# Feed-forward products of a one-layer encoder step: the Strassen sums of the weight blocks move to VectorE, with one cast and one low part per k pair, and product banks in pairs

## The chip, the cores and the metric

The kernel runs on one core of one Trainium2 chip. The metric is the device time of one execution in microseconds (us). The kernel before took 3003.22 us, the median of three runs (3001.64 to 3003.44).

The core's engines run beside each other, each through its own list of instructions: PE (TensorE, matrix products), DVE (VectorE), ACT (ScalarE) and POOL (GpSimd) for elementwise work, and SP (SyncE), which issues most DMA transfers. Products are summed in PSUM, which here is used as eight banks of 512 float32 values in each of 128 partitions; the other tiles are in SBUF, and what doesn't fit goes to DRAM and back.

## The reference, cut to what matters

One layer of a streaming encoder, for 512 frames of a new stream and 16 frames of each of 8 running streams: 640 tokens in all, in float32. D_MODEL is 2048, D_FF is 5632, FFN_CONV is 3.

```python
def conv_ffn(h, conv_past, w_up, conv_w, w_down):
    gp, val = jnp.split(h @ w_up, 2, axis=-1)
    gc, conv_new = causal_conv(gp, conv_past, conv_w)
    return (jax.nn.silu(gc) * val) @ w_down, conv_new

def layer(x, ...):
    proj = rmsnorm(x, norm_mix_g) @ w_in
    ...
    x = x + concatenate([o_gdn, o_fox, o_lru]) @ w_out
    f_out, ffn_conv_new = conv_ffn(rmsnorm(x, norm_ffn_g), ...)
    return x + f_out, ...
```

A final RMSNorm follows. The mixers' caches and states and the last rows of `gp` are outputs too. The change touches only the two products of `conv_ffn` and what stands around them.

## The kernel before

**Tiling.** Features lie on the partitions: a feature tile is 128 features of all 640 tokens, kept as two halves of 320 tokens (HALF). A float32 matrix is split into a high part, rounded to float32r, and a low part, the rest; a product is three matmuls: high by high, high by low, low by high.

**Strassen's scheme in Winograd's form.** The two feed-forward products are cut into 2 x 2 blocks: the weights A by pair of output feature tiles and half of the inputs (K), the operand B by half of K and half of the tokens. Instead of eight block products there are seven, P1 to P7, each of a sum of weight blocks (S1 to S4 and some blocks as they are) by a sum of operand blocks (T1 to T4 and some blocks as they are); sums of the seven give the four output blocks. One step along K is a *k pair*: a tile of each half of K. It takes 7 x 3 = 21 matmuls of a 128 x 128 weight block by 128 x 320 operand (L1077). `SEQP` gives their order as (product, weight block, operand block).

**A k pair's weights** (`wino_w`, L1034 to 1055). SP loads four blocks, 512 columns (`w`). Three sums of 128 columns are made on Pool (L1047, 1049, 1052) and one on DVE (L1048), in a tile `ws`; ACT casts the three blocks that are used as they are (384 columns, L1050) and the four sums (512 columns, L1053) to the high part `wh`; DVE makes the two low parts `wl` (L1051, L1054). `next_w` keeps three pairs prepared.

**An operand set** (`wino_x`, L1009 to 1032) is one k pair of the operand: four blocks of 320 columns in `f`, four sums on Pool (L1013 to 1016), then a cast on ACT and a low part on DVE in three steps, of 640, 960 and 640 columns. `yield` ends a step: the generators that make operand sets are worked off a step at a time between the k pairs of the products (`drive`).

**The up products** (`up`, 44 passes, here called *feature tiles* or *up tiles*: each makes a gate tile and a value tile, from 8 k pairs). The 8 operand sets are made once (`form0`). At a tile's end ACT copies P1 and DVE adds the other products to it (five adds of 320 columns, and for the gate, `gate`, two of 256 and two of 64, which put the tokens where the convolution wants them). Pool multiplies by `corr`, a correction to the norm's factor (128 x 656), the width-3 convolution runs on ACT (L253) and DVE (two operations, L257), silu on ACT (L1358), again `corr` on Pool (L1359), and four DVE products give the result, which Pool's queue stores to `hT` in DRAM.

**The down products** (`form`, `down`). `form` loads tiles of `hT` and makes operand sets, of which at most 8 are on the chip. So each pair of output feature tiles is visited several times: a *pass* takes the k pairs that have come since its last visit. There are 32 passes, four rounds over 8 output pairs; the first 8 passes have 2, 3, 3, 4, 5, 6, 7 and 8 k pairs, and the list `ends` sets the rest. A pass loads the two tiles of the running sum from `x2` (DRAM) on SP (L1402), accumulates its products in PSUM, and adds them: ACT copies P1 (L1416), DVE makes eight adds of 320 columns (L1412 six times, L1418, L1419), Pool three (the helper at L1415), and SP stores the two tiles back to `x2` (L1430). The last eight passes keep their results on the chip. The tiles of `x` in a pass come from a pool of four buffers.

**The tail.** `plain` takes the last of the k pairs without Strassen's scheme, 12 matmuls for a half of the tokens, adds them (L1459), and collects the sums of squares; `finish` makes the final norm.

**PSUM.** From the up products on, all eight banks are one pool of single banks (`pf`, L1304); a tile or a pass takes seven.

**What sets the order.** The program is written in a tile framework: a pool gives a tile a buffer, and the framework makes a writer wait until the last reader of that buffer is done. The framework's scheduler sets the order of each engine's instructions ahead of the run: by and large the order of the code, but an operation whose data come later can be put behind a few that the code issues after it (DVE, for example, makes one pair's sum ahead of the low parts of the pair before). On the chip each engine keeps to its order. SP issues loads and stores in order as well, so a load that waits for a buffer holds those behind it. What the code issues between what is set by `next_w` inside `wino`, by the steps of `form0` or `form` between the k pairs (three steps in the up products, one in the down passes), and by the adds of a pass, which come after its products.

Of the kernel before, what the change touches and what calls it, by code (L numbers as in the profile page):

```python
# [50 lines left out]
class K:  # L51
    def __init__(self, ctx, tc, a, cfg):
# [208 lines left out]
    def load_x(self):  # L261
        """x * g in two parts; and the sums of x squared; yields k tile by k tile"""
# [7 lines left out]
        # the first two feature tiles' weights between the tiles of x: the second one's at half the pace  # L270
# [11 lines left out]
        # the sums of squares run behind: the odd tiles' on Pool, the even ones' on ACT and DVE  # L282
# [26 lines left out]
    def gates(self, ps):  # L309
        """softplus-based gates of GDN and FoX, their running sums, in the forms that the mixers use"""  # L310
# [16 lines left out]
        # softplus(z), token-major: z (16 columns per token block), -lambda of the LRU (4 columns)  # L327
# [44 lines left out]
        # the caches' log forget values: their sums  # L372
# [15 lines left out]
        # chunk sums of the GDN gates, running sums of the FoX ones  # L388
# [7 lines left out]
        # token-major: beta and G of the heads  # L396
# [8 lines left out]
        # exp(G), -beta exp(G), beta / 2  # L405
# [6 lines left out]
        # G of the last token of its chunk, for each token  # L412
# [11 lines left out]
        # the FoX sums as three bfloat16 parts  # L424
# [17 lines left out]
    def parts3(self, outs, x, tmp):  # L442
        """outs: three bfloat16 parts whose sum is -x"""
# [8 lines left out]
    def gdn_in(self, h, f0):  # L452
        """projections and convolutions of head h: 2 silu(.) of q, k, v, and of z"""
# [31 lines left out]
    def gdn(self, h, y, zs):  # L485
# [6 lines left out]
        # token-major, normalised, and back  # L492
# [22 lines left out]
        # decays  # L515
# [33 lines left out]
        # M, then A^T  # L549
# [19 lines left out]
        # (I + M)^-1 by doubling blocks: X the inverse, Z its transpose  # L569
# [428 lines left out]
    def fb(self):  # L998
        return self.ffn.tile([P, 4, HALF], F32, tag="f", bufs=3, name=self.name("f"))
# [741 lines left out]
```

## Time and profile before

| | before |
|---|---|
| median of three runs | 3003.22 us (3001.64 to 3003.44) |
| the profiled execution: its span, first to last instruction | 3000.6 us, the one time of it that is on record |
| mean granted TensorE clock | 0.983 of full speed |
| high by high and high by low of the feed-forward products (L1077, `wh`) | 7280 matmuls |
| low by high (L1077, `wl`) | 3640 matmuls |
| HBM traffic over the span | 122 GB/s |

The profile is of one execution. Its page gives the busy time of each engine, then the span in 40 equal slices of 75 us, with the busy share of each in tenths; "PEclk" is the clock that TensorE was granted. PEld is TensorE's weight load, which runs beside its matmuls. A row of the trace names the line of the kernel, the engine, the operation, and the tiles that it writes and reads ("wl<-ws,wh"), with partitions x columns and the type. A row of waits has the time an engine waited ahead of a line, the line that it waited for, the total, the count and the longest wait, in us. Windows are stretches of the span, with the busy time and the count of instructions of each engine.

By time the kernel has these stages: the input projection, the mixers and the output projection to 1232 us; the start of the up products to 1300; the up products to 2320; the first down passes to 2460; the middle ones to 2800; the last ones to 2936; the tail to the end.

### The profile page before, as it was taken

How to read it: one execution, taken by the hardware profiler on the slowest of the kernel's cores; microseconds unless marked ns; L12 is line 12 of the kernel's file. 1: busy time of each engine (PE TensorE's matmuls, PEld its weight loads, DVE VectorE, ACT ScalarE, POOL GpSimd, SP SyncE). 2: the span in 40 equal slices, each digit the busy share in tenths (PEclk: the TensorE clock that was granted, in tenths of full speed). 3: DMA queues.
4: the chain of work that ended last, by engine and by line, in shares of the span. 5: the costliest groups of instructions: out<-in, count | busy, mean ns of one | idle time of the engine just before them, and what ended most of it. 6: DMA issues, size and time to landing. Idle time of an engine off the chain costs nothing. (4 is left out here: it accounts for less than half of the span.)

```text
span 3000.6 us, 54322 instructions
## 1 busy us (share of the span) xinstructions
PE 2888.2 (96%) x19927; PEld 2804.4 (93%) x19927; DVE 2315.5 (77%) x3976; ACT 1109.7 (37%) x2023; POOL 1631.7 (54%) x2367
## 2 busy tenths in 40 slices
PE   8999999999999999999999999999999789999997
PEld 7999999999999999999999999999999789999996
DVE  8746545645634537899999999999999988999888
ACT  4333323323322313444444443444444334434433
POOL 3312200310300014677777777777777988888775
PEclk9999999999999999999999999999999899999998
DMA  5123143134134745433333333333333555555443
GB/s 207 56 93 109 59 143 121 59 123 143 58 109 150 264 130 179 130 105 98 98 99 101 98 98 103 99 101 98 98 98 98 171 160 156 164 163 173 155 138 119
DMA packets 175772, 369.68 MB, mean 123 GB/s; under 512 B 20137, under 2 KB 25145, under 8 KB 175505
## 3 DMA queue, kind: packets, MB, share of 16 engines
q1 hardware_dynamic: 169088, 340.28, 36.4%
q0 software_dynamic: 6416, 25.94, 2.4%
q8 instruction: 156, 2.56, 0.4%
q14 instruction: 112, 0.91, 0.1%
HBM read 306.75 MB, written 59.39 MB: 122 GB/s over the span
## 5 line engine op out<-in xcount | busy, mean ns | idle before, releaser
L1077 PE MATMUL p<-x,wh 128*128 128x320 f32 x7280 | 1625.0, 312 | 45.0 <-DVE t L1412 31.9
L1077 PEld LDWEIGHTS p<-x,wh 128*128 128x128 f32 x7280 | 1230.5, 190 | 56.4 <-DVE t L1412 36.2
L1077 PE MATMUL p<-x,wl 128*128 128x320 f32 x3640 | 1138.9, 313 | 8.9 <-DVE wl L1054 5.2
L1077 PEld LDWEIGHTS p<-x,wl 128*128 128x128 f32 x3640 | 691.5, 190 | 19.9 <-DVE wl L1054 15.1
L1054 DVE TENSOR_TENSOR wl<-ws,wh 128x512 fp32r<-128x512 f32 x520 | 527.4, 1014 | 25.3 <-ACT wh L1053 25.2
L1051 DVE TENSOR_TENSOR wl<-w,wh 128x384 fp32r<-128x384 f32 x520 | 449.6, 865 | 73.4 <-ACT wh L1050 67.7
L1053 ACT CAST wh<-ws 128x512 fp32r<-128x512 f32 x520 | 321.6, 619 | 389.4 <-POOL ws L1052 340.1
L146 PE MATMUL d<-xh,whi 128*128 128x320 f32 x1536 | 396.8, 327 | 0.0
L1050 ACT CAST wh<-w 128x384 fp32r<-128x384 f32 x520 | 264.8, 509 | 330.0 <-issue 169.8
L1052 POOL TENSOR_TENSOR ws<-w,ws 128x128 f32<-128x128 f32 x520 | 352.7, 678 | 40.4
L146 PE MATMUL d<-xl,whi 128*128 128x320 f32 x1536 | 370.8, 310 | 0.0
L146 PE MATMUL d<-xh,wlo 128*128 128x320 f32 x1536 | 370.5, 310 | 0.0
L1047 POOL TENSOR_TENSOR ws<-w 128x128 f32<-128x128 f32 x520 | 284.1, 546 | 150.3 <-DVE wl L1054 144.0
L1049 POOL TENSOR_TENSOR ws<-ws,w 128x128 f32<-128x128 f32 x520 | 344.0, 662 | 37.5
L135 DVE TENSOR_TENSOR wlo<-raw,whi 128x512 fp32r<-128x512 f32 x230 | 175.1, 761 | 212.5 <-ACT whi L134 204.8
L134 ACT CAST whi<-raw 128x512 fp32r<-128x512 f32 x230 | 142.4, 619 | 405.9 <-PE d L146 354.1
L146 PEld LDWEIGHTS d<-xh,whi 128*128 128x128 f32 x1536 | 256.9, 190 | 9.5 <-issue 5.5
L146 PEld LDWEIGHTS d<-xl,whi 128*128 128x128 f32 x1536 | 262.6, 189 | 0.2 <-issue 0.2
L146 PEld LDWEIGHTS d<-xh,wlo 128*128 128x128 f32 x1536 | 262.7, 189 | 0.0
L1048 DVE TENSOR_TENSOR ws<-w 128x128 f32<-128x128 f32 x520 | 218.3, 426 | 13.2 <-DMA w<-in_w_down 0.7
L868 POOL COPY q<-t 128x128 f32<-128x128 f32 x24 | 12.1, 523 | 261.2 <-DVE t L220 139.8
L257 DVE SCALAR_TENSOR_TENSOR t<-t,prm,t 128x656 f32<-128x656 f32 (+1 forms) x136 | 138.4, 1017 | 6.5 <-ACT t L253 3.5
(395 smaller groups left out, 3513.5 us busy)
## 6 DMA issues: line engine op xcount, KB each, us to landing
w<-in_w_up SPq DMA_DIRECT2D x352, 256.0 KB, 2.6
raw<-in_w_in SPq DMA_DIRECT2D x196, 256.0 KB, 2.8
w<-in_w_down SPq DMA_DIRECT2D x184, 256.0 KB, 2.7
t<-x SPq DMA_DIRECT2D x74, 320.0 KB, 3.6
kc<-in_ckT SPq DMA_DIRECT2D x32, 512.0 KB, 5.0
vc<-in_cv SPq DMA_DIRECT2D x32, 512.0 KB, 5.8
x<-t SPq DMA_DIRECT2D x48, 320.0 KB, 2.2
hT<-t POOLq DMA_DIRECT2D x44, 320.0 KB, 2.5
```

The lines of the kernel that those rows point to most:

```text
L134: nc.scalar.copy(hi[:, :n], raw[:, :n])
L135: nc.vector.tensor_sub(lo[:, :n], raw[:, :n], hi[:, :n].bitcast(F32))
L146: self.nc.tensor.matmul(ps[h][:, :HALF], wt[:, w], x[:, h * HALF:(h + 1) * HALF], start=start and i == 0, stop=stop and i == 2)
L1047: nc.gpsimd.tensor_add(s[:, 0], w[:, 0], w[:, 3])
L1048: nc.vector.tensor_sub(s[:, 2], w[:, 1], w[:, 0])
L1049: nc.gpsimd.tensor_sub(s[:, 1], s[:, 0], w[:, 1])
L1050: nc.scalar.copy(hi[:, 0:3], w[:, 1:4])
L1051: nc.vector.tensor_sub(lo[:, 0:3], w[:, 1:4], hi[:, 0:3].bitcast(F32))
L1052: nc.gpsimd.tensor_sub(s[:, 3], w[:, 2], s[:, 1])
L1053: nc.scalar.copy(hi[:, 3:7], s)
L1054: nc.vector.tensor_sub(lo[:, 3:7], s, hi[:, 3:7].bitcast(F32))
L1077: nc.tensor.matmul(ps[p], l[:, wi], r[:, xi], start=i == 0 and j == 0, stop=i == n - 1 and j == 2)
```

## The change

Seven products are still made for each k pair, of the same sizes and number of matmuls. What changes is who makes the sums, in how many operations, and in which PSUM banks the products lie.

- The scheme has other signs, so that two of the weight sums have a common minuend: one DVE operation of 256 columns makes both, and two DVE operations of 128 columns the other two. Pool makes none. The sums lie in the same tile as the loaded blocks (`w` now has 8 blocks, `ws` is gone), so that one ACT cast of 896 columns and one DVE low part of 896 columns serve all seven.
- `next_w` prepares sums and cast of a pair when it makes the low part of the pair before (`wn`).
- An operand set has its blocks and sums in one tile `f` of 7 blocks (two buffers, where there were three of 4 blocks and each set took two); cast and low part come in two steps, of 1280 and 960 columns, with a `yield` after each of the four operations.
- PSUM is split into four single banks (`pf1`: P1, P6, P7, the tail, and the other uses) and two tiles of two banks (`pf2`: P4 with P5, P2 with P3).
- In a down pass one tile with one buffer (`x2`, 128 x 1280) holds both tiles of the running sum, loaded by one DMA and stored by one. DVE's eight adds of 320 columns become four of 320 and two of 640; Pool's three become one of 640 and one of 320.
- The load of the convolution's past rows (`fc0`) is split into four; the host lays two weight blocks in another order; the number of bytes for DMA descriptors (`dynamic_dma_scratch_size`) is set to 4096. Comments and docstrings go, which shifts the line numbers.

```diff
-    SEQP = ((1, 0, 0), (6, 4, 5), (7, 5, 6), (5, 3, 4), (2, 1, 2), (4, 2, 1), (3, 6, 3))
+    SEQP = ((1, 0, 5), (6, 5, 1), (7, 3, 2), (5, 4, 0), (4, 1, 6), (2, 2, 3), (3, 6, 4))
     def fb(self):
-        return self.ffn.tile([P, 4, HALF], F32, tag="f", bufs=3, name=self.name("f"))
+        return self.ffn.tile([P, 7, HALF], F32, tag="f", bufs=2, name=self.name("f"))
...
     def pf1(self):
-        return self.pf.tile([P, 512], F32, tag="p", name=self.name("p"))
+        return self.pf.tile([P, 512], F32, tag="p", bufs=4, name=self.name("p"))
+    def pf2(self):
+        return self.pf.tile([P, 1024], F32, tag="pp", bufs=2, name=self.name("pp"))
     def wino_x(self, f, ready=lambda: True):
-        t = self.fb()
-        nc.gpsimd.tensor_sub(t[:, 0], f[:, 1], f[:, 0])
-        nc.gpsimd.tensor_sub(t[:, 1], f[:, 3], t[:, 0])
-        nc.gpsimd.tensor_sub(t[:, 2], f[:, 3], f[:, 1])
-        nc.gpsimd.tensor_sub(f[:, 1], f[:, 2], t[:, 1])
+        nc.gpsimd.tensor_sub(f[:, 0], f[:, 6], f[:, 5])
+        nc.gpsimd.tensor_add(f[:, 1], f[:, 4], f[:, 0])
+        nc.gpsimd.tensor_add(f[:, 2], f[:, 4], f[:, 6])
+        nc.gpsimd.tensor_sub(f[:, 6], f[:, 3], f[:, 1])
...
-        nc.scalar.copy(h3[:, 2:4], f[:, 2:4])
-        nc.vector.tensor_sub(l3[:, 2:4], f[:, 2:4], h3[:, 2:4].bitcast(F32))
-        yield
-        nc.scalar.copy(h3[:, 4:7], t[:, 0:3])
-        nc.vector.tensor_sub(l3[:, 4:7], t[:, 0:3], h3[:, 4:7].bitcast(F32))
-        yield
-        nc.scalar.copy(h3[:, 0:2], f[:, 0:2])
-        nc.vector.tensor_sub(l3[:, 0:2], f[:, 0:2], h3[:, 0:2].bitcast(F32))
+        for a, b in ((3, 7), (0, 3)):
+            nc.scalar.copy(h3[:, a:b], f[:, a:b])
+            yield
+            nc.vector.tensor_sub(l3[:, a:b], f[:, a:b], h3[:, a:b].bitcast(F32))
+            yield
     def wino_w(self, src, plain):
-        w = self.wf.tile([P, 4, P], F32, tag="w", bufs=4, name=self.name("w"))
-        s = None if plain else self.wf.tile([P, 4, P], F32, tag="ws", bufs=2, name=self.name("ws"))
+        w = self.wf.tile([P, 8, P], F32, tag="w", bufs=4, name=self.name("w"))
...
-        nc.gpsimd.tensor_add(s[:, 0], w[:, 0], w[:, 3])
-        nc.vector.tensor_sub(s[:, 2], w[:, 1], w[:, 0])
-        nc.gpsimd.tensor_sub(s[:, 1], s[:, 0], w[:, 1])
-        nc.scalar.copy(hi[:, 0:3], w[:, 1:4])
-        nc.vector.tensor_sub(lo[:, 0:3], w[:, 1:4], hi[:, 0:3].bitcast(F32))
-        nc.gpsimd.tensor_sub(s[:, 3], w[:, 2], s[:, 1])
-        nc.scalar.copy(hi[:, 3:7], s)
-        nc.vector.tensor_sub(lo[:, 3:7], s, hi[:, 3:7].bitcast(F32))
-        return hi, lo
+            nc.vector.tensor_tensor(w[:, 4:6], w[:, 0:1].to_broadcast([P, 2, P]), w[:, 1:3], op=OP.subtract)
+            nc.vector.tensor_sub(w[:, 6], w[:, 1], w[:, 5])
+            nc.vector.tensor_sub(w[:, 7], w[:, 3], w[:, 6])
+            part = w[:, 1:8]
+        n = part.shape[1]
+        nc.scalar.copy(hi[:, 0:n], part)
+        return part, hi, lo
+    def wino_lo(self, part, hi, lo):
+        n = part.shape[1]
+        self.nc.vector.tensor_sub(lo[:, 0:n], part, hi[:, 0:n].bitcast(F32))
+        return hi, lo
     def next_w(self):
         while len(self.wq) < 3:
-            src = next(self.wseq, None)
-            if src is None:
+            if self.wn is None:
+                src = next(self.wseq, None)
+                self.wn = src and self.wino_w(*src)
+            if self.wn is None:
                 break
-            self.wq.append(self.wino_w(*src))
+            now, src = self.wn, next(self.wseq, None)
+            self.wn = src and self.wino_w(*src)
+            self.wq.append(self.wino_lo(*now))
         return self.wq.pop(0)
     def wino(self, n, xops, make=None, base=0, done=None):
-        ps = {p: self.pf1()[:, :HALF] for p, _, _ in self.SEQP}
+        one = {p: self.pf1() for p in (1, 6, 7)}
+        two = [self.pf2().rearrange("p (a c) -> p a c", a=2) for _ in range(2)]
+        ps = {p: t[:, :HALF] for p, t in one.items()}
+        ps[45], ps[23] = [t[:, :, :HALF] for t in two]
+        for p, t in ((4, 45), (5, 45), (2, 23), (3, 23)):
+            ps[p] = ps[t][:, p % 2 if t == 23 else p - 4]
...
-        nc.gpsimd.dma_start(ns_fc[:, :, 1:, :], a["fc0"])
+        for f in range(0, NF, 11):
+            nc.gpsimd.dma_start(ns_fc[:, f:f + 11, 1:, :], a["fc0"][:, f:f + 11])
...
         def down(i, end, make):
             last = end == nw
+            xx = k.xt() if last else k.ffn.tile([P, 2 * NTOK], F32, tag="x2", bufs=1, name=k.name("x2"))
             if last:
-                fin[i] = k.xt()
-            xs = [fin[i][:, e * NTOK:(e + 1) * NTOK] if last else k.t() for e in range(2)]
-            for e in range(2):
-                nc.sync.dma_start(xs[e], x2[2 * i + e])
+                fin[i] = xx
+            x = xx[:, :2 * NTOK].rearrange("p (e h c) -> p e h c", e=2, h=2)
+            nc.sync.dma_start(x.rearrange("p e h c -> p e (h c)"), x2[2 * i:2 * i + 2].rearrange("e p t -> p e t"))
...
-            add(0, 0, ps[1])
+            nc.vector.tensor_add(x[:, 0, 0], x[:, 0, 0], ps[1])
             nc.vector.tensor_add(u2, u2, ps[6])
             nc.vector.tensor_add(u3, u2, ps[7])
-            add(0, 1, ps[5])
-            add(1, 1, ps[5])
-            add(0, 0, ps[2])
-            add(1, 0, ps[4])
-            add(0, 1, ps[3])
-            gadd(1, 1, u3)
-            gadd(1, 0, u3)
-            gadd(0, 1, u2)
+            nc.vector.tensor_add(x[:, 1], x[:, 1], ps[45])
+            nc.vector.tensor_add(x[:, 0, 1], x[:, 0, 1], ps[5])
+            nc.vector.tensor_add(x[:, 0], x[:, 0], ps[23])
+            nc.gpsimd.tensor_tensor(x[:, 1], x[:, 1], u3.unsqueeze(1).to_broadcast([P, 2, HALF]), op=OP.add)
+            nc.gpsimd.tensor_add(x[:, 0, 1], x[:, 0, 1], u2)
             if not last:
-                for e in range(2):
-                    nc.sync.dma_start(x2[2 * i + e], xs[e])
+                nc.sync.dma_start(x2[2 * i:2 * i + 2].rearrange("e p t -> p e t"), x.rearrange("p e h c -> p e (h c)"))
```

More of the change, by code (lines that the diff above doesn't have):

```diff
@@ L988, in load_o, with fpart @@
             yield
-    SEQP = ((1, 0, 0), (6, 4, 5), (7, 5, 6), (5, 3, 4), (2, 1, 2), (4, 2, 1), (3, 6, 3))
+    SEQP = ((1, 0, 5), (6, 5, 1), (7, 3, 2), (5, 4, 0), (4, 1, 6), (2, 2, 3), (3, 6, 4))
     def fb(self):
-        return self.ffn.tile([P, 4, HALF], F32, tag="f", bufs=3, name=self.name("f"))
+        return self.ffn.tile([P, 7, HALF], F32, tag="f", bufs=2, name=self.name("f"))
+    @staticmethod
+    def fpart(f, j):
+        return f[:, 5 - 2 * j:7 - 2 * j, :].rearrange("p a c -> p (a c)")
     def xt(self, dt=F32):
@@ L1037, in wino_w @@
         nc = self.nc
[L1038 to L1039 removed]
+        w = self.wf.tile([P, 8, P], F32, tag="w", bufs=4, name=self.name("w"))
         hi = self.wf.tile([P, 7, P], F32R, tag="wh", bufs=3, name=self.name("wh"))
         lo = self.wf.tile([P, 7, P], F32R, tag="wl", bufs=3, name=self.name("wl"))
[L1042 removed]
+        nc.sync.dma_start(w[:, 0:4].rearrange("p a c -> p (a c)"), src)
         if plain:
[L1044 to L1054 removed]
+            part = w[:, 0:4]
+        else:
+            nc.vector.tensor_tensor(w[:, 4:6], w[:, 0:1].to_broadcast([P, 2, P]), w[:, 1:3], op=OP.subtract)
[8 more added lines that the diff above has]
+        self.nc.vector.tensor_sub(lo[:, 0:n], part, hi[:, 0:n].bitcast(F32))
         return hi, lo
@@ L1303, in body @@
         k.mix = k.ffn
-        k.pf = ctx.enter_context(tc.tile_pool(name="pf", bufs=8, space=PSUM, reuse_waits="tile"))
+        k.pf = ctx.enter_context(tc.tile_pool(name="pf", bufs=4, space=PSUM, reuse_waits="tile"))
         def spread(r, out):
@@ L1389, in form @@
                 hi, lo = [x[:, :4 * HALF].rearrange("p (a c) -> p a c", c=HALF) for x in op]
-                nc.scalar.copy(hi, f)
+                nc.scalar.copy(hi, f[:, 3:7])
                 yield
-                nc.vector.tensor_sub(lo, f, hi.bitcast(F32))
+                nc.vector.tensor_sub(lo, f[:, 3:7], hi.bitcast(F32))
                 hops.append((hi, lo))
@@ L1408, in down @@
             u2, u3 = u[:, :HALF], u[:, HALF:NTOK]
-            x = {(e, h): xs[e][:, h * HALF:(h + 1) * HALF] for e in range(2) for h in range(2)}
-            def add(e, h, b):
-                nc.vector.tensor_add(x[e, h], x[e, h], b)
-            def gadd(e, h, b):
-                nc.gpsimd.tensor_add(x[e, h], x[e, h], b)
             nc.scalar.copy(u2, ps[1])
-            add(0, 0, ps[1])
+            nc.vector.tensor_add(x[:, 0, 0], x[:, 0, 0], ps[1])
             nc.vector.tensor_add(u2, u2, ps[6])
             nc.vector.tensor_add(u3, u2, ps[7])
-            add(0, 1, ps[5])
-            add(1, 1, ps[5])
-            add(0, 0, ps[2])
-            add(1, 0, ps[4])
-            add(0, 1, ps[3])
-            gadd(1, 1, u3)
-            gadd(1, 0, u3)
-            gadd(0, 1, u2)
+            nc.vector.tensor_add(x[:, 1], x[:, 1], ps[45])
[3 more added lines that the diff above has]
+            nc.gpsimd.tensor_add(x[:, 0, 1], x[:, 0, 1], u2)
             if not last:
-                for e in range(2):
-                    nc.sync.dma_start(x2[2 * i + e], xs[e])
+                nc.sync.dma_start(x2[2 * i:2 * i + 2].rearrange("e p t -> p e t"), x.rearrange("p e h c -> p e (h c)"))
         blocks = (0, 128, HALF - 128)
@@ L1451, in plain @@
                     n = 0
-                    for kh, wi in enumerate(((1, 2), (0, 3))[e]):
+                    for kh, wi in enumerate(((1, 3), (0, 2))[e]):
                         for l, r in ((hi, xh), (hi, xl), (lo, xh)):
-                            nc.tensor.matmul(ps[e], l[:, wi], r[:, 2 * kh + h], start=n == 0, stop=n == 5)
+                            nc.tensor.matmul(ps[e], l[:, wi], r[:, 2 - 2 * kh + h], start=n == 0, stop=n == 5)
                             n += 1
@@ L1511, in weights @@
                     yield a["w_down"][i, nw], True
-        k.wseq, k.wq = weights(), []
+        k.wseq, k.wq, k.wn = weights(), [], None
         for f in range(NF - 1):
```

14 lines of the change are left out of this document (5 added, 9 removed).

## The prediction

> **What bounds the kernel now.** I read the page first, for shares and slices.
>
> ```profile
> span 3000.6 us, 54322 instructions
> PE 2888.2 (96%) x19927; PEld 2804.4 (93%) x19927; DVE 2315.5 (77%) x3976; ACT 1109.7 (37%) x2023; POOL 1631.7 (54%) x2367
> PE   8999999999999999999999999999999789999997
> DVE  8746545645634537899999999999999988999888
> POOL 3312200310300014677777777777777988888775
> PEclk9999999999999999999999999999999899999998
> ```
>
> PE is full almost everywhere; the one dip (slices 32 and 33) has a lower granted clock and a Pool at nine and eight tenths. Next the windows by stage: start of the up products, up products, first down passes, middle ones, last ones, tail.
>
> ```profile
> 1232.00:1300.00 68.00, 62.30 (x409) 60.55 (x409) 60.73 (x104) 31.50 (x54) 54.25 (x81) 0.97 0.31 92
> 1300.00:2320.00 1020.00, 1017.64 (x6878) 1008.53 (x6878) 970.17 (x1598) 412.08 (x777) 785.99 (x1273) 1.00 0.34 100
> 2320.00:2460.00 140.00, 112.78 (x658) 107.06 (x657) 129.08 (x189) 56.08 (x99) 126.42 (x156) 0.89 0.51 165
> 2460.00:2800.00 340.00, 319.99 (x2081) 314.00 (x2080) 305.00 (x459) 137.48 (x253) 288.02 (x392) 0.97 0.52 161
> 2800.00:2936.00 136.00, 136.00 (x930) 136.00 (x929) 115.87 (x207) 49.98 (x96) 97.36 (x151) 1.00 0.45 144
> ```
>
> After the stretch and its length stand PE, weight loads, DVE, ACT and Pool with their counts, then the clock. The up products run 6878 matmuls in 1020 us, 6.74 a us. At that rate the first down passes would hold 944 and have 658: 42.4 us lost. The middle ones would hold 2293 and have 2081: 31.4 us lost. The start loses 7.3 us. So some 81 us can be won in these stages; up and last passes hold PE at its own pace. The waits of PE between 2320 and 2800 say what ends last:
>
> ```profile
> PE p L1077 <- DVE t L1412: 31.9, 16, 3.5
> PE p L1077 <- ACT wh L1050: 5.1, 3, 2.3
> ```
>
> At 16 pass ends PE waits 2.0 us for the adds that free the product banks, so DVE is behind. The loss has two parts: PE idle, 27.2 and 20.0 us by the windows, and the clock that drops after a stop, 0.11 x 140 = 15 and 0.03 x 340 = 10 us. So a stop that goes takes half its length again with it. DVE is behind because it shares its time with Pool:
>
> ```profile
> 1817.37 1.86 POOL L1354 TENSOR_TENSOR t<-t,corr 128x656 f32<-128x656 f32 x1 [1.55 <-DVE t L1344]
> 1817.67 2.10 DVE L1054 TENSOR_TENSOR wl<-ws,wh 128x512 fp32r<-128x512 f32 x1
> ```
>
> An operation that takes 0.68 at best (below) lasted until Pool's was done.
>
> **Costs of one operation.** Minimum, median, maximum by line:
>
> ```profile
> L1048 DVE TENSOR_TENSOR ws<-w x520: 276/433/970, 1216.4 to 2924.1; 128x128 f32<-128x128 f32 x174
> L1051 DVE TENSOR_TENSOR wl<-w,wh x520: 543/812/1760, 1226.5 to 2929.3; 128x384 fp32r<-128x384 f32 x174
> L1054 DVE TENSOR_TENSOR wl<-ws,wh x520: 676/946/2114, 1227.0 to 2930.3; 128x512 fp32r<-128x512 f32 x174
> L1412 DVE TENSOR_TENSOR t<-t,p x144: 472/475/482, 2363.6 to 2838.9; 128x320 f32<-128x320 f32 x144
> L1047 POOL TENSOR_TENSOR ws<-w x520: 446/506/1369, 1216.2 to 2924.4; 128x128 f32<-128x128 f32 x174
> L1014 POOL TENSOR_TENSOR f<-f,f x29: 857/1169/1460, 1152.5 to 2772.3; 128x320 f32<-128x320 f32 x29
> L1359 POOL TENSOR_TENSOR t<-t,corr x44: 1338/1344/1352, 1279.7 to 2366.1; 128x656 f32<-128x656 f32 x44
> L1463 POOL TENSOR_TENSOR x<-x,t x10: 1540/1606/2011, 2945.0 to 2972.5; 128x640 f32<-128x640 f32 x10
> ```
>
> DVE's minima lie on 143 ns + 1.042 ns a column. Four rows give the spacing (start, duration): independent neighbours start 0.39 apart at 0.48 long, so 0.09 overlaps; an operation that waits for the one before starts 0.04 after its end.
>
> ```profile
> 2938.70 0.48 DVE L1412 TENSOR_TENSOR x<-x,p 128x320 f32<-128x320 f32 x1
> 2939.09 0.48 DVE L1419 TENSOR_TENSOR u<-u,p 128x320 f32<-128x320 f32 x1
> 2984.68 0.16 DVE L114 TENSOR_TENSOR s<-s 128x3 f32<-128x3 f32 x1
> 2984.88 0.16 DVE L115 SCALAR_TENSOR_TENSOR s<-s,s 128x3 f32<-128x3 f32 x1
> 2934.96 0.31 PE L1077 MATMUL p<-x,wl 128*128 128x320 f32 x1
> 2935.40 0.31 PE L1077 MATMUL p<-x,wl 128*128 128x320 f32 x1
> ```
>
> The last two are three matmuls apart: 0.1467 each, 3.08 us for the 21 of a k pair, 24.64 for a feature tile of 8 pairs.
>
> **Weight blocks, per k pair.** Removed: three Pool sums (3 x 0.446 = 1.34 us undisturbed), one DVE sum and two low parts (0.276 + 0.543 + 0.676 - 3 x 0.09 = 1.225). Added on DVE: a sum of 256 columns (no such row; 0.41 by the line, between the 128 and 384 rows' 0.276 and 0.543), two of 128, one low part of 896 columns (1.08 by the line, beyond its longest row; the two removed ones together were 1.22). That is 2.04 us of durations. The second and third sum each wait for the one before. DVE in the steady part of an up tile, before:
>
> ```order
> L1048 TENSOR_TENSOR ws_18666<-w_18665 128x128
> L1051 TENSOR_TENSOR wl_18634<-w_18631,wh_18633 128x384
> L1054 TENSOR_TENSOR wl_18634<-ws_18632,wh_18633 128x512
> L1048 TENSOR_TENSOR ws_18700<-w_18699 128x128
> L1051 TENSOR_TENSOR wl_18668<-w_18665,wh_18667 128x384
> L1054 TENSOR_TENSOR wl_18668<-ws_18666,wh_18667 128x512
> ```
>
> and now (w holds the blocks and their sums, wl the low part):
>
> ```order
> L1051 TENSOR_TENSOR w_16918<-w_16918 128x256
> L1052 TENSOR_TENSOR w_16918<-w_16918 128x128
> L1053 TENSOR_TENSOR w_16918<-w_16918 128x128
> L1061 TENSOR_TENSOR wl_16860<-w_16858,wh_16859 128x896
> L1051 TENSOR_TENSOR w_16948<-w_16948 128x256
> L1052 TENSOR_TENSOR w_16948<-w_16948 128x128
> ```
>
> Here the waiting sums follow directly; elsewhere others stand between. Taken as half and half: 2.04 - 3 x 0.09 + 0.04 = 1.80 us, between 1.68 (none adjacent) and 1.94 (all). So DVE alone gets 0.58 us more per pair, Pool 1.34 less. What Pool costs DVE decides.
>
> **Up products.** The other DVE work of a tile is 15 operations (five adds of 320 columns, two each of 256 and 64, the conv's two of 656, four products of 256 and 64), by the line and the spacing 5.3 us. Before: 8 x 1.225 + 5.3 = 15.1 alone; Pool 8 x 1.34 + 3.6 (two of 656 columns at 1.34, and 0.9 put down for small copies) = 14.3; DVE was busy 970/1020 of 24.64 = 23.4. So a share (23.4 - 15.1)/14.3 = 0.58 of Pool's time lands on DVE. After: 8 x 1.80 + 5.3 + 0.58 x 3.6 = 21.8, with all of Pool's time 23.3: below 24.64 either way. PE stays the bound: -1 us (it idles 2.4 in the stage).
>
> At a tile's end the banks go in pairs: P4 and P5 come free together after five adds, P2 and P3 after the gate's. PE after three products of a new tile, before:
>
> ```order
> L1077 MATMUL p_19412<-x_11700,wh_19315 128x320
> L1077 MATMUL p_19412<-x_11701,wh_19315 128x320
> L1077 MATMUL p_19412<-x_11700,wl_19316 128x320
> L1077 MATMUL p_19413<-x_11700,wh_19315 128x320
> L1077 MATMUL p_19413<-x_11701,wh_19315 128x320
> ```
>
> and now:
>
> ```order
> L1094 MATMUL p_18644<-x_11859,wh_18557 128x320
> L1094 MATMUL p_18644<-x_11860,wh_18557 128x320
> L1094 MATMUL p_18644<-x_11859,wl_18558 128x320
> L1094 MATMUL p_18645<-x_11859,wh_18557 128x320
> L1094 MATMUL p_18645<-x_11860,wh_18557 128x320
> L1094 MATMUL p_18645<-x_11859,wl_18558 128x320
> L1094 MATMUL p_18646<-x_11859,wh_18557 128x320
> L1094 MATMUL p_18646<-x_11860,wh_18557 128x320
> L1094 MATMUL pp_18647<-x_11702,wh_18527 128x320
> ```
>
> Instead of the fourth product stand eight matmuls of the second pair's single products, so the paired bank (pp) is wanted 17 x 0.147 = 2.5 us into the tile. P1 ends 2.6 us before the old tile does, and seven adds and two sums of about 0.4 each run from then: done at about +1.2, or +2.2 with a low part in front. Covered; uncovered, each 0.5 us of lateness would cost 43 x 0.5 = 21 us.
>
> **Middle down passes.** Counts in a stage, by the windows of one line: low parts (pairs), the second u sum (passes) and the 960-column low part (operand sets), then the pairs of the first passes.
>
> ```profile
> 2460.00:2800.00 340.00, 82.03 (x99) 0.97 0.52 161
> 2460.00:2800.00 340.00, 7.14 (x15) 0.97 0.52 161
> 2460.00:2800.00 340.00, 15.08 (x13) 0.97 0.52 161
> 2320.00:2460.00 140.00, 26.17 (x32) 0.89 0.51 165
> ```
>
> Operands of a set: one cast less, low parts 1.48 + 1.14 - 0.18 = 2.44 on DVE for 2.49; two more turns between steps, hidden, since a set is used for the first time only every sixth pair or so. Adds of a pass: eight of 320 (3.1 us) become four and two of 640 (0.81 by the line): 3.0. Pool's three adds of 0.87 become 1.54 + 0.87. Before, as pairs + passes + sets: DVE alone 99 x 1.225 + 15 x 3.1 + 13 x 2.49 = 200, Pool alone 99 x 1.34 + 15 x 2.6 + 13 x 3.43 = 216 (four sums of 0.857 a set), busy 305: share (305 - 200)/216 = 0.49. After: DVE 99 x 1.80 + 15 x 3.0 + 13 x 2.44 = 255; Pool 15 x 2.4 + 45 = 81. DVE: 255 + 0.49 x 81 = 294, between 255 and 336. PE needs 305. DVE was filled to 0.90; without Pool's chain in front of the casts I take 0.95, 310 us, and leave 8 us for stops: 318, **-22 us**.
>
> **First down passes** (32 pairs, 6 passes, 8 sets and the last tile's 5.3 us). Before, casts stood behind Pool:
>
> ```profile
> 2335.09 0.99 ACT L1027 CAST x<-f 128x960 fp32r<-128x960 f32 x1 [7.04 <-POOL f L1014]
> ```
>
> That wait goes with the weight sums that stood ahead on Pool. By the same sum DVE alone was 83 and Pool 90, busy 129 (share 0.51). Now DVE alone is 32 x 1.71 (few sums adjacent here) + 18 + 19.5 + 5.3 = 97 and Pool 14.5 + 27.5 + 3.6 = 46: 97 + 0.5 x 46 = 120, between 97 and 143; filled to 0.95 that is 127 for 140. Against it: x2 has one buffer, so a pass's x is loaded only after the last one's is stored.
>
> ```profile
> x<-t SPq DMA_DIRECT2D x48, 320.0 KB, 2.2
> t<-x SPq DMA_DIRECT2D x74, 320.0 KB, 3.6
> vc<-in_cv SPq DMA_DIRECT2D x32, 512.0 KB, 5.8
> ```
>
> Adds 2.4, Pool 2, store 2.2 to 4, load 3.6 to 6: 10 to 14 us a round. Passes of 6 pairs (18.5 us) cover it, those of 3, 3 and 4 pairs (9.2, 9.2, 12.3) don't: 0 to 11 us, partly inside DVE's 127. Behind the waiting load SP holds the weight loads, but it runs some six pairs ahead, which covers 14 us; behind an add that waits for x DVE holds the next pairs' sums and low parts, and PE waits for those. I take 5 of the 13 back: **-8 us**.
>
> **The rest.** Start: Pool's chain gone, -2 (-7 to +5). Last passes: 45 pairs x 1.80 + 9 x 3.0 + 0.4 x 22 of Pool's adds = 117 us of DVE, for 116 now, in 136: 0. Tail: single banks fall from 8 to 4, so PE can be only one pair ahead.
>
> ```profile
> 2947.09 0.87 DVE L1459 TENSOR_TENSOR x<-x,p 128x320 f32<-128x320 f32 x2
> 2947.88 1.27 DVE L1045 TENSOR_TENSOR wl<-w,wh 128x512 fp32r<-128x512 f32 x1
> 2949.07 0.87 DVE L1459 TENSOR_TENSOR x<-x,p 128x320 f32<-128x320 f32 x2
> ```
>
> DVE takes 1.98 us a pair, PE 12 x 0.147 = 1.76; tied together for 16 pairs: +4 (0 to +8). ACT's casts shrink and wait less; ACT is never the bound. Splitting the fc0 load and the smaller descriptor ring touch nothing on the path: 0.
>
> Sum: -2 - 1 - 8 - 22 + 4 = -29; 3000.6 - 29 = 2971.6. The median lies 2.6 above the profiled span: **2974 us**.
>
> **Rivals.**
> A (0.60): the sum above; its own range 2955 to 2992.
> B (0.14): PE becomes the bound in the down passes too, as DVE's 294 for 305 allows: -42 - 31 - 5 - 1 + 2 = -77: 2926. Against it: DVE stays above 0.9.
> C (0.12): the pass ends are late as before, since their adds are no shorter and DVE is as full: 2997 to 3009.
> D (0.14), slower: all of Pool's time lands on DVE. Filled to 0.97, the middle takes 336/0.97 = 346 (+6), the first passes 143/0.97 + 8 = 155 (+15), tail +6: 3000.6 + 27 + 2.6 = 3030. Break-even over both stages, at a fill of 0.95 and with the +4 and -3 of the rest: (479 x 0.95 - 255 - 97)/(81 + 46) = a share of 0.81; the stages show 0.49 to 0.58, which is why D gets no more.
> The Trainium skill, SBUF — State Buffer, "Who interferes with whom", speaks for D: a DVE instruction with two SBUF inputs and a GpSimd instruction that reads SBUF exclude each other, and the second to issue is fully blocked. The rows of 1817 agree; the shares stay below 1 since Pool also runs beside adds that read PSUM.
>
> A change under 0.2% (6 us) can't be told from none. Faster A and B: 0.74; same C: 0.12; slower D: 0.14. The range reaches halfway from A into D and most of the way to B: 2935 to 3016.
>
> **What would show it.** Right: up stage at 6.7 matmuls a us with DVE near 0.9; low part near 1.08 us; middle near 318 us. Wrong: a DVE pair above 2.4 us, PE waits on paired banks in the up tiles, or PE waits after x loads.

## The result and the profile after

The changed kernel took 3034.47 us (median of four runs, 3032.94 to 3035.66) where the kernel before took 3003.33: a ratio of 1.0104, 95% interval 1.009 to 1.0118. It is 1% slower; 2974 had been forecast, with a range that ended at 3016.

First the page of the changed kernel: span, engines, and three rows of slices.

```profile
span 3033.9 us, 51647 instructions
PE 2888.9 (95%) x19927; PEld 2794.8 (92%) x19927; DVE 2281.2 (75%) x4403; ACT 1048.3 (35%) x1474; POOL 727.1 (24%) x778
PE   7999999999999998999999999999999789999996
DVE  8746545644643537898889888898898998999887
POOL 3312200300310013222222223222222433322114
```

Pool has lost 905 of its 1632 us. DVE, which took over its sums, is no busier than before (2281 for 2316). PE does the same matmuls in the same busy time, and the span is 33 us longer: PE waits more. Next the windows by stage, cut where PE starts the same matmul as at the cuts of before (there at 1232.1, 1300.1 and 2936.1 in place of the round times), so each holds the same products as the rows in the prediction. The columns are again length, PE, weight loads, DVE, ACT, Pool, clock.

```profile
1237.80:1302.80 65.00, 61.38 (x409) 60.47 (x408) 58.46 (x118) 28.36 (x33) 16.98 (x25) 0.97 0.33 95
1302.80:2338.80 1036.00, 1020.38 (x6878) 1008.39 (x6877) 923.02 (x1926) 378.45 (x450) 255.43 (x292) 1.00 0.34 98
2338.80:2473.20 134.40, 109.89 (x658) 104.55 (x657) 124.79 (x198) 50.65 (x59) 60.26 (x54) 0.91 0.47 159
2473.20:2818.00 344.80, 317.05 (x2082) 308.06 (x2081) 311.33 (x519) 124.77 (x142) 93.47 (x76) 0.99 0.49 160
2818.00:2967.30 149.30, 139.59 (x930) 136.15 (x930) 127.30 (x226) 44.83 (x54) 24.94 (x20) 1.00 0.43 136
```

Against before: +5.7 us ahead of the first cut, -3 in the start, **+16.1 in the up products**, -5.6 in the first down passes, +4.8 in the middle ones, **+13.2 in the last ones** (136.1 before, with no idle time of PE at all), +2.1 in the tail. In none of the three long stages is DVE full: 923 of 1036, 311 of 345, 127 of 149. The waits of PE in the changed kernel (total, times, longest) say what it lacks; line 1369 is an add at a tile's end in `up`, lines 1427 to 1432 are the adds of a down pass, "pp" is a pair of banks:

```profile
PE pp L1094 <- DVE x L1432: 21.4, 26, 1.0
PE p L1094 <- DVE x L1427: 16.6, 11, 4.4
PE pp L1094 <- DVE t L1369: 11.6, 20, 1.2
PE pp L1094 <- DVE x L1431: 7.9, 15, 0.6
```

All four are banks that come free late, three of them paired ones. One tile's end on DVE and PE (start, duration, line; DVE's sums of 128 columns are left out). Its last stop is one of the longer ones: PE waits for line 1369 at 20 tile ends, 0.6 us each on average.

```profile
1821.75 0.43 DVE L1051 TENSOR_TENSOR w<-w 128x256 f32<-128x256 f32 x1 [2.09 <-DMA w<-in_w_up]
1822.75 1.08 DVE L1061 TENSOR_TENSOR wl<-w,wh 128x896 fp32r<-128x896 f32 x1
1823.75 0.42 DVE L1051 TENSOR_TENSOR w<-w 128x256 f32<-128x256 f32 x1
1824.74 1.08 DVE L1061 TENSOR_TENSOR wl<-w,wh 128x896 fp32r<-128x896 f32 x1
1825.74 0.48 DVE L1364 TENSOR_TENSOR t<-t,p 128x320 f32<-128x320 f32 x1
...
1828.68 0.48 DVE L1369 TENSOR_TENSOR t<-t,pp 128x320 f32<-128x320 f32 x1
```

```profile
1824.76 0.45 PE L1094 MATMUL p<-x,wh 128*128 128x320 f32 x2
1826.28 0.55 PE L1094 MATMUL p<-x,wh 128*128 128x320 f32 x2 [0.47 <-DVE t L1364]
1829.21 0.56 PE L1094 MATMUL pp<-x,wh 128*128 128x320 f32 x2 [1.06 <-DVE t L1369]
```

PE begins the new tile at 1824.76. DVE, which stood idle for 2.09 us up to 1821.75 because the weights of a later pair had not landed, then makes sums and low part of two later pairs, and comes to the first add 1.0 us *after* the old tile has ended. PE stops twice, 1.5 us in this tile. The same at the end of a down pass, DVE and Pool, then PE:

```profile
2655.78 0.47 DVE L1431 TENSOR_TENSOR x<-x,pp 128x320 f32<-128x320 f32 x1
2656.18 2.26 DVE L1061 TENSOR_TENSOR wl<-w,wh 128x896 fp32r<-128x896 f32 x1
2658.36 0.81 DVE L1432 TENSOR_TENSOR x<-x,pp 128x640 f32<-128x640 f32 x1
```

```profile
2655.94 1.55 POOL L1433 TENSOR_TENSOR x<-x,u 128x640 f32<-128x640 f32 x1 [1.28 <-DVE u L1429]
```

```profile
2656.40 0.53 PE L1094 MATMUL pp<-x,wh 128*128 128x320 f32 x2 [0.58 <-DVE x L1431]
2659.32 0.53 PE L1094 MATMUL pp<-x,wh 128*128 128x320 f32 x2 [0.78 <-DVE x L1432]
```

The last add, which frees P2 and P3, stands behind the low part of a later pair, and that one takes 2.26 us beside Pool's add where it takes 1.08 elsewhere. PE waits 0.6 us for one pair of banks and 0.8 us for the other. Of the 32 pass ends it waits for line 1432 at 26 and for line 1431 at 15.

### The profile page after: what moved, and what is told of

It reads as the page before. It is cut to its first block, busy times and chain, and to the rows that moved or that the text cites. A ratio compares the mean times of both kernels' runs of the same rounds, so it can differ in the third digit from the quotient of the medians.

```text
span 3033.9 us, 51647 instructions
## 1 busy us (share of the span) xinstructions
PE 2888.9 (95%) x19927; PEld 2794.8 (92%) x19927; DVE 2281.2 (75%) x4403; ACT 1048.3 (35%) x1474; POOL 727.1 (24%) x778
## 4 chain that ended last, share of the span: by engine, by line
DVE 23%; PE 20%; DMA 8%; issue 4%; POOL 4%; ACT 1%; DVEq 0%; SPq 0%; ACTq 0%; POOLq 0%
PE pp L1094 11%; DVE wl L1061 8%; PE p L1094 7%; DMA w<-in_w_up 5%; DMA w<-in_w_down 3%; DVE w L1051 3%; DVE w L1052 2%; POOL t L1371 2%; DVE w L1053 1%; POOL t L1376 1%; DVE t L257 1%; DVE x L1036 1%; DVE x L1432 1%; DVE t L1360 1%; ACT t L253 1%
## 5 line engine op out<-in xcount | busy, mean ns | idle before, releaser
L1094 PE MATMUL pp<-x,wh 128*128 128x320 f32 x4160 | 934.3, 311 | 42.0 <-DVE x L1432 21.4
L1056 ACT CAST wh<-w 128x896 fp32r<-128x896 f32 (+1 forms) x536 | 495.8, 932 | 849.9 <-PE pp L1094 477.8
L1094 PEld LDWEIGHTS pp<-x,wh 128*128 128x128 f32 x4160 | 694.7, 188 | 63.2 <-issue 38.8
L1094 PE MATMUL p<-x,wh 128*128 128x320 f32 x3120 | 705.5, 312 | 30.0 <-DVE x L1427 16.6
L1094 PE MATMUL pp<-x,wl 128*128 128x320 f32 x2080 | 643.2, 309 | 0.0
L1061 DVE TENSOR_TENSOR wl<-w,wh 128x896 fp32r<-128x896 f32 (+1 forms) x536 | 616.6, 1151 | 20.2 <-ACT wh L1056 14.8
L1094 PEld LDWEIGHTS p<-x,wh 128*128 128x128 f32 x3120 | 527.0, 190 | 37.4 <-DVE x L1427 20.3
L1094 PE MATMUL p<-x,wl 128*128 128x320 f32 x1560 | 486.5, 312 | 8.6 <-DVE wl L1061 8.6
L1094 PEld LDWEIGHTS p<-x,wl 128*128 128x128 f32 x1560 | 296.7, 190 | 10.5 <-DVE wl L1061 10.5
L1053 DVE TENSOR_TENSOR w<-w 128x128 f32<-128x128 f32 x520 | 239.8, 465 | 8.4
L1052 DVE TENSOR_TENSOR w<-w 128x128 f32<-128x128 f32 x520 | 161.9, 316 | 7.5
```

The costliest lines, as they stand in the source:

```text
L1052: nc.vector.tensor_sub(w[:, 6], w[:, 1], w[:, 5])
L1053: nc.vector.tensor_sub(w[:, 7], w[:, 3], w[:, 6])
L1056: nc.scalar.copy(hi[:, 0:n], part)
L1061: self.nc.vector.tensor_sub(lo[:, 0:n], part, hi[:, 0:n].bitcast(F32))
L1094: nc.tensor.matmul(ps[p], l[:, wi], r[:, xi], start=i == 0 and j == 0, stop=i == n - 1 and j == 2)
```

## The experiments

Theory 1: banks in pairs come free late. Theory 2: Pool's operations stretch those of DVE. Theory 3: the one x2 buffer delays the adds or the loads. Each run below is a median of four (ten for the adds first on the kernel before), with its ratio to the kernel before.

**Single banks.** The changed kernel with eight single banks:

```diff
-    one = {p: self.pf1() for p in (1, 6, 7)}          (and two pairs from pf2)
+    ps = {p: self.pf1()[:, :HALF] for p, _, _ in self.SEQP}
-    nc.vector.tensor_add(x[:, 1], x[:, 1], ps[45])
+    nc.vector.tensor_add(x[:, 1, 0], x[:, 1, 0], ps[4])
+    nc.vector.tensor_add(x[:, 1, 1], x[:, 1, 1], ps[5])      (P2 and P3 likewise)
```

> The changed kernel with all eight PSUM banks single again, and in a down pass an add of 320 columns for each bank in place of the two of 640. Theory 1 (paired banks come free late, and TensorE stops for them at the ends of tiles and passes): the up products get back 12 to 16 us of their 16, the middle and last passes 15 to 30 us; 2990 to 3008 us. Theory 2 (Pool's operations stretch those of VectorE, whatever the banks are): within 6 us of the changed kernel's 3034. Theory 3 (the single x2 buffer delays the adds): within 6 us of 3034.

Measured 2985.9 us, ratio 0.9938 (0.9923 to 0.9953): 48.6 us less than the changed kernel, more than theory 1 had put down (2990 to 3008), and faster than before. Theories 2 and 3 fall as the main cause. Up, middle and last stage:

```profile
1305.30:2321.20 1015.90, 1012.38 (x6877) 1008.30 (x6877) 898.22 (x1925) 386.87 (x451) 247.05 (x293) 1.00 0.35 100
2450.40:2782.90 332.50, 315.90 (x2082) 310.99 (x2081) 301.06 (x550) 125.95 (x142) 97.31 (x78) 0.98 0.53 168
2782.90:2919.00 136.10, 136.10 (x930) 136.09 (x930) 121.42 (x246) 45.05 (x54) 31.21 (x20) 1.00 0.47 148
```

The up products give back 20 us, the last passes all 13. In the middle PE still idles 16.6 us.

**The adds first.** Banks in pairs, but the sums and low parts that the code issues after a tile's or pass's adds are kept behind these adds on DVE:

```diff
+    k.behind = nc.vector.tensor_add(x[:, 0], x[:, 0], ps[23]).ins        (in up: the gate's last add)
+    with tc.issue_after(k.behind):        # order on the engine alone, no wait
         nc.vector.tensor_sub(lo[:, 0:n], part, hi[:, 0:n].bitcast(F32))   (and the three sums)
```

> The changed kernel, banks in pairs, but on VectorE the weight sums and low parts that the code issues after the adds of a tile or pass stand behind these adds (order alone, no other work). Theory 1 in the form that the order on VectorE makes the banks late: the stop for P2 and P3 (0.8 us at some 24 pass ends) goes, and part of the 16 us of the up products: 3004 to 3018 us. Theory 1 in the form that pairing alone does it: 3026 to 3036. Theories 2 and 3: 3026 to 3036.

Measured 2990.27 us, ratio 0.9956 (0.9941 to 0.997): 44.2 us less, with pairs of banks and not one operation fewer, and well past the range of theory 1's form for the order (3004 to 3018). So it is not the pairing alone: what stands ahead of the adds makes the banks late. Up, middle and last stage:

```profile
1306.30:2335.20 1028.90, 1023.02 (x6877) 1008.31 (x6877) 895.75 (x1923) 382.70 (x451) 266.32 (x293) 1.00 0.34 99
2471.90:2787.20 315.30, 309.47 (x2082) 306.23 (x2081) 289.00 (x516) 124.90 (x142) 90.74 (x74) 0.99 0.56 174
2787.20:2923.80 136.60, 136.45 (x930) 136.07 (x930) 120.02 (x228) 44.38 (x54) 26.39 (x20) 1.00 0.47 149
```

The middle passes fall by 29.5 us, below the run with single banks, and the last ones by 12.7; the up products by only 7.1, and why PE's busy time there is 10.6 us above that with single banks, for the same matmuls, was not settled.

**Both.** The two edits together.

> Single banks and the adds first on VectorE, both edits together on the changed kernel. If the late start of the adds (a low part and sums of later pairs ahead of them) is a cause of its own beside the pairing: the 15 us that TensorE still stops for the first add in the middle passes of the run with single banks go, the up products stay at their 1016 us: 2964 to 2974 us. If the two edits remove the same stops: 2982 to 2990.

Measured 2973.26 us, ratio 0.9904 (0.9887 to 0.992): the first case. Its five stages:

```profile
1236.70:1302.40 65.70, 61.63 (x408) 60.47 (x408) 58.73 (x116) 27.72 (x33) 17.20 (x25) 0.97 0.31 91
1302.40:2320.70 1018.30, 1015.60 (x6878) 1008.47 (x6877) 891.83 (x1923) 383.55 (x452) 266.54 (x293) 1.00 0.35 100
2320.70:2450.80 130.10, 107.02 (x659) 101.72 (x658) 119.90 (x209) 49.30 (x57) 60.65 (x50) 0.93 0.49 157
2450.80:2770.60 319.80, 311.26 (x2081) 305.06 (x2081) 294.23 (x550) 125.78 (x142) 94.95 (x79) 1.00 0.56 174
2770.60:2906.90 136.30, 136.30 (x929) 136.02 (x928) 121.94 (x249) 44.34 (x54) 25.79 (x20) 1.00 0.49 150
```

| median, us | order as it came | adds first |
|---|---|---|
| banks in pairs | 3034.47 (the change) | 2990.27 |
| single banks | 2985.90 | 2973.26 |

Pairs cost 48.6 us in the order that came and 17.0 with the adds first; the order costs 44.2 with pairs and 12.6 without. Late adds and pairs that come free only with the last of several adds make one another worse. By stage, pairs with the adds first lose 10.6 us in the up products, 6.6 in the first passes and 3.8 ahead of the start; in the middle passes they cost nothing (315.3 us for 319.8).

**Pool's adds after DVE's.** In a down pass Pool's two adds swapped, so that both wait for line 1432:

```diff
-    nc.gpsimd.tensor_tensor(x[:, 1], x[:, 1], u3..., op=OP.add)
     nc.gpsimd.tensor_add(x[:, 0, 1], x[:, 0, 1], u2)
+    tc.keep_in_program_order(nc.gpsimd.tensor_tensor(x[:, 1], x[:, 1], u3..., op=OP.add))
```

> The changed kernel with Pool's two adds of a down pass swapped, so that both start after the last add of VectorE. Theory 2: the low part that stands ahead of the last add falls from 2.25 to about 1.1 us, the stop for P2 and P3 from 0.8 to 0 us at some 24 pass ends, and the time by 12 to 20 us: 3014 to 3022. Theory 1 with the order alone: the low part stays ahead of the add, but the add is 1.2 us earlier all the same, so the same forecast for the stop if the low part shrinks, and no change (3030 to 3036) if it keeps its length beside no Pool work.

Measured 3029.37 us, ratio 1.0093 (1.0072 to 1.0113). The same place in the pass:

```profile
2653.34 1.08 DVE L1061 TENSOR_TENSOR wl<-w,wh 128x896 fp32r<-128x896 f32 x1
2654.34 0.81 DVE L1432 TENSOR_TENSOR x<-x,pp 128x640 f32<-128x640 f32 x1
```

The low part is back at 1.08 us, and PE no longer waits for line 1432: theory 2 is right on the mechanism. It is wrong on the price, 5 us for 12 to 20, which the intervals don't separate from none. Pool's adds now run beside the sums that come next, and PE waits longer for the first add of a pass:

```profile
2656.44 1.86 DVE L1052 TENSOR_TENSOR w<-w 128x128 f32<-128x128 f32 x2
```

```profile
PE p L1094 <- DVE x L1427: 22.0, 16, 3.7
```

Two sums of 128 columns take 1.86 us there (one alone takes 0.28), while Pool's add of 640 columns runs from 2656.19 to 2657.94. The waits for line 1427 are 22.0 us, for 16.6 in the changed kernel, and those for line 1431 are 15.3, for 7.9: most of the loss moved to these.

**Pairs on the kernel before.** Its weight blocks stay; banks and adds as in the change, and the order of two products with them.

> The kernel before with banks in pairs as in the changed kernel (P4 with P5, P2 with P3, and the adds of 640 columns), its weight blocks left as they were. Theory 1 (a pair of banks comes free late whatever prepares the weights): up products +10 to +20, last passes +6 to +13, middle +5 to +15: 3024 to 3048 us. If only the new order of VectorE's work makes the pairs late: 2998 to 3010.

Measured 3022.93 us, ratio 1.0067 (1.0052 to 1.0082), just under the range of theory 1: pairs cost 20 us on the old weight blocks too. The stages lie under the low ends of that theory too (up products +7.9, middle +3.9, last passes +5.3): on that kernel pairs cost less than half of the 48.6 us that they cost in the change. Line 1420 there is the helper for adds of 320 columns in a pass; the first row is for a single bank, the second for the pair of P4 and P5:

```profile
PE p L1085 <- DVE t L1420: 24.9, 15, 4.5
PE pp L1085 <- DVE t L1420: 11.3, 13, 0.9
```

**The adds first on the kernel before.** The same rule of order, nothing else.

> The kernel before, with its own weight sums on Pool, and only the order on VectorE changed: its sums and low parts that the code issues after a pass's or tile's adds stand behind them. Theory a (the order alone is worth the gain, the new weight blocks nothing): 2975 to 2990 us. Theory b (the load that the new weight blocks take off is what counts, VectorE is late there by load): 2994 to 3006.

Measured 3000.59 us, ratio 0.999 (0.9981 to 0.9999): theory b. With Pool's chain in front of the casts and 305 us of DVE in the middle passes, order gives 2 us. So the gain of the run with both edits needs what the change does to weight blocks and operand sets; these two were not run apart.

**The sums on Pool.** Single banks, adds first, and the three operations that make a pair's four sums on Pool (in the kernel before, three of the four were):

```diff
-    nc.vector.tensor_tensor(w[:, 4:6], w[:, 0:1].to_broadcast([P, 2, P]), w[:, 1:3], op=OP.subtract)
+    nc.gpsimd.tensor_tensor(w[:, 4:6], w[:, 0:1].to_broadcast([P, 2, P]), w[:, 1:3], op=OP.subtract)
```

> Single banks and the adds first (the run at 2973 us), with the three weight sums of a k pair on Pool in place of VectorE; one cast and one low part as they are. Theory a (the sums are better on VectorE, since half of Pool's time lands on VectorE anyway, and the cast no longer waits for Pool): the middle passes go from 320 to some 335 us, VectorE in them from 294 to 305 or more: 2984 to 3003 us. Theory b (one cast and one low part are the gain, and who makes the sums does not matter): 2966 to 2979.

Measured 3155.99 us, ratio 1.0505 (1.049 to 1.0521): the side of theory a, but at six times the top of its price. The up stage and the middle passes, and the three operations:

```profile
1307.30:2365.20 1057.90, 1023.41 (x6877) 1010.25 (x6877) 676.15 (x943) 378.19 (x451) 963.13 (x1278) 1.00 0.32 96
2522.50:2936.40 413.90, 347.04 (x2081) 335.90 (x2081) 219.80 (x243) 122.46 (x138) 317.90 (x366) 0.90 0.39 131
```

```profile
L1051 POOL TENSOR_TENSOR w<-w 128x256 f32<-128x256 f32 x520 | 485.1, 933 | 127.1 <-DMA w<-in_w_down 111.2
L1053 POOL TENSOR_TENSOR w<-w 128x128 f32<-128x128 f32 x520 | 398.5, 766 | 40.7
L1052 POOL TENSOR_TENSOR w<-w 128x128 f32<-128x128 f32 x520 | 360.5, 693 | 37.3
```

A pair's sums take Pool 2.39 us of the 3.08 that PE needs. In the up products Pool, with `corr` and the copies on top, is busy 963 of 1058 us, and DVE only 676. But the up products lose 40 us of the 183; the middle passes lose 94, and there Pool is busy 318 of 414 us, so it is not full. Of theory a's two reasons the first isn't seen: DVE holds 220 us of the middle, where 305 or more had been expected. The second is: the casts wait 249 us of these 414 for Pool's last sum, and sums, cast and low part of a pair stand in series across three engines. That this series is the cause in the middle is the likely reading and was not taken apart. With one cast for all seven blocks, sums on DVE are worth 183 us.

**The running sum in two tiles.** First on the changed kernel, then on the run with both edits: two tiles from the pool of four buffers, two loads and two stores. The one tile with two buffers in place of one, the nearer test, has no room in SBUF: a pool allocated after it (`xpb`) takes 52.5 KB a partition, and 49.3 would be left.

> The changed kernel with the running sum of a pass in two tiles of the pool of four buffers, two loads and two stores, as in the kernel before, in place of the one x2 tile with one buffer; adds and banks unchanged. Theory 3 (the single buffer's round trip costs): 3020 to 3029 us. Theory 1: within 5 us of 3034, since no add of VectorE waits for x in the changed kernel's trace.

> Single banks and the adds first, with the running sum of a pass in two tiles of the pool of four buffers, as in the kernel before. Theory 3 (the single x2 buffer costs in the first, short passes): the first passes go from 130 to 122 to 127 us: 2964 to 2971 us. Otherwise 2971 to 2976.

Measured 3028.33 us, ratio 1.008 (1.0065 to 1.0095), and 2964.29 us, ratio 0.9865 (0.985 to 0.988): 6 and 9 us. Theory 3 holds as a small cost. On the first kernel the intervals of the two ratios overlap; on the second they don't. First and middle passes of the second:

```profile
2318.80:2445.20 126.40, 108.34 (x658) 103.39 (x657) 118.72 (x210) 48.50 (x57) 58.66 (x50) 0.92 0.54 175
2445.20:2757.00 311.80, 308.17 (x2082) 305.02 (x2081) 289.98 (x551) 125.80 (x142) 98.06 (x79) 1.00 0.56 179
```

3.7 us of it is in the short passes, where it was expected, and 8 in the middle ones, where it was not. This is the fastest version of the study.

**The loaded blocks first.** On the run with both edits, an operand set's casts in three steps of which the first doesn't wait for Pool's sums; then the same together with the two tiles.

```diff
-    for a, b in ((3, 7), (0, 3)):        (a yield after each cast and each low part)
+    for a, b in ((3, 6), (0, 3), (6, 7)):        (cast and low part together; a yield after the first two)
```

> Single banks and the adds first, with the casts of an operand set in three steps again, the three loaded blocks first (960, 960 and 320 columns), so that the first cast of a set does not wait for Pool's sums. If the 5 us lost ahead of 1232 us come from casts that stand on ScalarE behind Pool's sums and ahead of the out-projection's weight casts: that stretch ends at 1232 to 1233 us, not 1237 to 1240, and the time is 2966 to 2971. If they come from elsewhere: 2972 to 2976.

> The two edits of the other runs together: three steps of an operand set with the loaded blocks first, and the running sum in two tiles, on single banks with the adds first. If both gains hold and add up: 2958 to 2967 us. If only one holds: 2966 to 2972.

Measured 2973.29 us, ratio 0.9895 (0.988 to 0.991), and 2968.43, ratio 0.9877 (0.9861 to 0.9894): no gain in either. What was expected of ScalarE is seen, in the changed kernel and then here:

```profile
1190.68 0.99 ACT L1034 CAST x<-f 128x960 fp32r<-128x960 f32 x1 [7.42 <-POOL f L1024]
```

```profile
1186.75 0.99 ACT L1034 CAST x<-f 128x960 fp32r<-128x960 f32 x1 [6.54 <-DVE f L1207]
```

The cast that stood behind Pool's sums, with the out-projection's weight casts behind it, no longer waits for them, though it still waits 6.54 us for DVE. The first cut, where the start of the up products begins, is at 1233.7 us, for 1236.7; with the two tiles as well it is at 1235.7, for 1234.9. The middle passes took 9 us more in both runs, which also have another number of steps in a set. So the loss ahead of 1232 us is explained in part at most.

## Why the prediction was wrong

| span, us, against before | forecast | the change | single banks | pairs, adds first | single banks, adds first |
|---|---|---|---|---|---|
| ahead of the start | 0 | +5.7 | +7.1 | +8.4 | +4.6 |
| start | -2 | -3.0 | -1.9 | -2.2 | -2.3 |
| up products | -1 | +16.1 | -4.0 | +9.0 | -1.6 |
| first down passes | -8 | -5.6 | -10.8 | -3.3 | -9.9 |
| middle passes | -22 | +4.8 | -7.5 | -24.7 | -20.2 |
| last passes | 0 | +13.2 | 0.0 | +0.5 | +0.2 |
| tail | +4 | +2.1 | -0.1 | +0.1 | +0.8 |

**What failed is the step on the paired banks.** "Covered; uncovered, each 0.5 us of lateness would cost 43 x 0.5 = 21 us." It let the seven adds run from the end of P1, 2.6 us before the tile's end, behind two sums and at most a low part. In the trace sums and low parts of two later pairs stand ahead, the first add starts 1.0 us after the tile's end, and the bank is free at 1829.2, 4.4 us after the tile's end instead of 1.2 to 2.2, where the prediction had it wanted at 2.5. The up products lost 16.1 us, 0.37 us a tile, and single banks gave 20 back. "PE waits on paired banks in the up tiles" was among the prediction's own signs of being wrong.

**The pass ends had no such term at all.** The prediction priced the adds of a pass as work (3.1 us, then 3.0), not by when each bank comes free. Of the 27.7 us that PE idles in the middle, 16.9 are waits for pairs and 10.8 for the first add of a pass; in the last passes, where it had "117 us of DVE, for 116 now, in 136" and no loss, 9.6 of 9.7 are waits for pairs. Either edit brings the last passes back. In the middle the order weighs more: the -22 that became +4.8 is -24.7 with the adds first and pairs kept, and -7.5 with single banks and the order as it came. A DVE that is not full was taken for one that is in time.

**What stays open is the part of the weight loads.** In the tile shown, the two pairs' sums came late ahead of the adds because DVE, in order, had waited for weights to land. The prediction took SP's loads to run some six pairs ahead; ahead of DVE they don't. DVE waits so 114 times for up weights in the changed kernel (first row), never in the kernel before, and nearly as often with single banks (second row):

```profile
DVE w L1051 <- DMA w<-in_w_up: 59.4, 114, 2.4
DVE w L1051 <- DMA w<-in_w_up: 55.4, 108, 2.4
```

With single banks the up products lose nothing by it, so these waits alone are not the cause. How much they add where banks are in pairs no run shows, since none gives `w` another buffer.

**The weight blocks were priced right.** Without pairs and with the adds first, the middle passes hold 294.2 us of DVE (294 forecast) and last 319.8 (318 forecast), the first passes 119.9 and 130.1 (120, and 132), and the median is 2973.26 for a forecast of 2974. The low part of 896 columns takes 1.08 us, as the line said. That agreement has luck in it: the tail and the stretch ahead of the start miss by 3 and 5 us with opposite signs, and the x2 round trip cost 8 us in the middle, where no term stood for it. DVE's 294 is itself made of two misses that cancel: Pool was busy 95 us there, not 81, and (294 - 255)/95 = 0.41 of that landed on DVE, not 0.49. The clock's share did not hold either: a stop was to cost "half its length again", but in the change the middle has 27.7 us of idle PE at a granted clock of 0.99, where before it had 20.0 at 0.97.

**The rivals.** D was the one on the right side, and its 3030 us lies 4 us from the measured time by luck: it filled DVE with Pool's time in the down passes, put +15 us on the first passes, which gained 5.6, and nothing on the up and last passes, which lost 29. DVE holds 311 of 345 us in the middle passes, so (311 - 255)/93 = 0.60 of Pool's time landed on it, short of the break-even of 0.81. C came closer in mechanism, the pass ends late as before, but it knew no price for pairs and so stopped at no change. At a pass end the low part, with two SBUF inputs, starts 0.24 us after Pool's add, lasts 2.26 us, and ends 0.95 us after that add; with the add moved away it lasts 1.08. The rule of the Trainium skill, SBUF — State Buffer, "Who interferes with whom", that such an operation contends with a GpSimd one that reads SBUF, agrees with the trace. The contention matters here through the place where it strikes, ahead of the last add, and not through the sum of Pool's time.

**Ahead of the start**, 5.7 us were lost that no step looked at, and 4.6 to 8.4 in the three runs of the table. One candidate is seen in a row: an operand set's cast stands behind Pool's sums and in front of the out-projection's on ScalarE. Undoing it gave 3 us in one run and none in the other; the rest stays open.

## What to carry to other kernels

An accumulator that is widened to two banks comes free with the last add that reads either bank, so its price is read at the tile's end: when the bank is wanted, which instructions stand ahead of the add on its in-order engine, and how long the longest of them gets beside other engines. A stage's load says how full an engine is and nothing on whether it is in time there. Where an engine has slack but releases late, putting the releases ahead of the preparation adds no operation: here it was worth 44 us with the banks in pairs, 13 with single banks, and 2 on the kernel before.

## What the runs showed of the hardware

An operation on DVE that reads two SBUF tiles stretched beside one of Pool's by much of the Pool operation's length: a low part from 1.08 to 2.26 us beside an add of 1.55. Pool's side stretches too: in the run with the sums on Pool, a sum of 128 columns that takes 0.46 us in other places took 1.42 beside a low part that started 0.02 us after it. An add of 640 columns from two PSUM banks takes 0.81 us, where two of 320 take 0.87 with their overlap (0.39 + 0.48): merging saves 0.06 us of work, and pairs cost 17 us even with the adds first.
